# Turning a decoder layer's gated activations with 32x32 block transposes and a way through DRAM instead of TensorE

## The chip, the cores and the metric

The kernel runs on one core of a Trainium2 chip. The metric is the device time of one execution in microseconds; lower is better. The engines are named as in the profile: PE (TensorE, with its weight loads as PEld), DVE (VectorE), ACT (ScalarE), POOL (GpSimd) and SP (SyncE, which here only issues DMAs).

## The reference, cut to what matters

One decoder layer over 256 tokens of width 2048, all in float32. It has two gated feed-forward half-steps, one ahead of and one behind a mixing part (windowed attention and a gated linear recurrence):

```python
def swiglu(h, w_gu, w_down):
    gate, up = jnp.split(h @ w_gu, 2, axis=-1)
    return (jax.nn.silu(gate) * up) @ w_down

x = x + 0.5 * swiglu(rmsnorm(x, ffn1_norm[l]), ffn1_w_gu[l], ffn1_w_down[l])
...                                   # mixing
x = x + 0.5 * swiglu(rmsnorm(x, ffn2_norm[l]), ffn2_w_gu[l], ffn2_w_down[l])
```

The inner width F is 5632. The change touches only what lies between `silu(gate) * up` and the product with `w_down`.

## The kernel before, in words

**Parts.** A float32 matrix product is made of three matmuls in float32r. Each operand is split into a high part (a copy rounded to float32r) and a low part (the rest), and the kernel adds high by high, high by low and low by high. `split_next` (L150, L151) splits the weights: ACT copies `w_raw` to `w_hi`, DVE subtracts to get `w_lo`. The weights come as chunks of 1 MB, 128 x 2048 elements, in a fixed order (`plan`); SP's queue loads them into four `w_raw` buffers, and there are two buffers each of `w_hi` and `w_lo`. `take` hands a chunk to the matmuls and sees to it that the chunk behind it has been split and that four more are on the way. So the split of chunk n+1 can begin when PE has left chunk n-1.

**Projections.** `project` runs over its chunks; for each it goes over the two halves of the tokens (t = 0 and 1, 128 tokens each) and issues 12 matmuls of 512 columns for each half, 24 in a chunk (`mm`, L94). Behind each half it calls `tick()`, so a projection of 8 chunks has 16 ticks. A tick takes one entry of the list `deferred` and runs it; `nothing` is an entry that does nothing. At the end of a projection `flush` runs what is left.

**Feed-forward.** `ffn` has 11 groups of 512 gate and 512 up columns. Each group is one projection `f_gu` of 8 chunks, at the end of which four PSUM banks hold gate and up for the two halves. For each half ACT computes silu of the gate (`sg`, L350) and DVE multiplies with the up part (`act_nat`, L352), tokens on the partitions. The down projection `f_d` needs these activations turned, with the inner width on the partitions, and split into parts (`f_ah`, `f_al`), which stay in SBUF for all 11 groups. `put_later` defers that into the next projection: its first tick does nothing, the second and third each run `put_two`, with four PE transposes of 128x128 into one bank of PSUM (L122), an ACT cast to the high part (L300) and a DVE subtraction to the low part (L301). Behind the last group the next projection is `f_d` itself, whose chunks 20 and 21 of 22 are the first to read that group. There are two feed-forward blocks, `f1` and `f2`, so 22 groups.

**Order.** Instructions are placed on the engines in the order of the program, with a list scheduler that may let one that is ready go ahead of one that waits for data or a buffer; each engine then runs its own in the fixed order that results. `tc.issue_after(ins)` keeps what is issued under it behind `ins` where both are on the same engine; it adds no wait between engines. `last["copy"]` and `last["rest"]` are the latest `w_hi` copy and `w_lo` subtraction that were issued.

**Buffers.** The pool `t2` has six buffers of 128x512 for passing values (`sg`, `act_nat`, the old residual, pieces of the rotary tables and of the mixing part).

Of the kernel before, what the change touches and what calls it, by code (L numbers as in the profile page):

```python
# [8 lines left out]
F32 = mybir.dt.float32  # L9
# [3 lines left out]
ALU = mybir.AluOpType  # L13
AX = mybir.AxisListType

P = 128
D = 2048
S = 256
T = S // P
# [37 lines left out]
def tile_layer(  # L57
# [8 lines left out]
    out = out[0]  # L66
    VE, SC, GP, PE = nc.vector, nc.scalar, nc.gpsimd, nc.tensor
# [10 lines left out]
    def s4(name, dtype=F32, shape=(P, 1024)):  # L78
        return s4p.tile(list(shape), dtype, name=name, tag="s4")

    def t2(name, shape=(P, 512)):
        return t2p.tile(list(shape), F32, name=name, tag="t2")
# [8 lines left out]
    last = {}  # L91
# [76 lines left out]
    deferred, queues = [], []  # L168
# [19 lines left out]
    def plan_project(name, w, c0, ncols, nk):  # L188
        per = 2048 // ncols
        for kc in range(nk // per):  # L190
            src = w[kc * per * P:(kc + 1) * per * P, c0:c0 + ncols].rearrange("(j p) c -> p j c", p=P)
            plan.append((name, [(src, 2048)]))

    def project(name, ncols, nk, xh, xl, near_end=None):

        per = 2048 // ncols
        nb = (ncols + 511) // 512
        wd = min(512, ncols)
        bk = [[bank(f"{name}_{t}_{i}") for i in range(nb)] for t in range(T)]
        chunks = nk // per  # L200
        for kc in range(chunks):
            hi, lo = take(name)
            for t in range(T):
                tok = slice(t * P, (t + 1) * P)

                order = [(range(per), [i]) for i in range(nb)] if kc == chunks - 1 else \
                    [([j], range(nb)) for j in range(per)]
                for js, bs in order:
                    for j in js:
                        k = kc * per + j  # L210
                        ah, al = xh(k)[:, tok], xl(k)[:, tok]
                        cols = {i: slice(j * ncols + i * 512, j * ncols + i * 512 + wd) for i in bs}
                        for i in bs:
                            mm(bk[t][i][:, :wd], ah, hi[:, cols[i]], k == 0, False)
                            mm(bk[t][i][:, :wd], ah, lo[:, cols[i]], False, False)
                        for i in bs:
                            mm(bk[t][i][:, :wd], al, hi[:, cols[i]], False, k == nk - 1)
                tick()
            if kc == chunks - 3 and near_end is not None:
                near_end()  # L220
        flush()
        return bk
# [89 lines left out]
    def put_two(parts, k0, nat, kp, gain=None):  # L312
        ps = trb("put_ps")
        for j in range(2):
            for t in range(T):
                c = (2 * kp + j) * P
                transpose(ps[:, j * S + t * P:j * S + (t + 1) * P], nat[t][:, c:c + P])
        parts.put(k0 + 2 * kp, 2, ps, gain)

    def put_later(parts, k0, nat):  # L320
        deferred.extend([nothing, lambda: put_two(parts, k0, nat, 0), lambda: put_two(parts, k0, nat, 1)])

    def plan_ffn(name, w_gu, w_down):
        guv = w_gu.rearrange("d (h f) -> d h f", h=2)
        for g in range(F // 512):
            for kc in range(KT // 2):
                if not plan:

                    plan.append((f"{name}_gu", [
                        (guv[j * P:(j + 1) * P, h, :512], 512) for j in range(2) for h in range(2)]))  # L330
                    continue
                plan.append((f"{name}_gu", [
                    (guv[(kc * 2 + j) * P:(kc * 2 + j + 1) * P, :, g * 512:(g + 1) * 512], 1024)
                    for j in range(2)]))
        for cg in range(2):
            plan_project(f"{name}_d", w_down, cg * 1024, 1024, F // P)

    def ffn(name, h, old, done):

        act = Parts(f"{name}_act", 0)  # L340
        for g in range(F // 512):
            act.hi.append(s4(f"{name}_ah", F32R, (P, 4, S)))
            act.lo.append(s4(f"{name}_al", F32R, (P, 4, S)))
            bk = project(f"{name}_gu", 1024, KT, h.xh, h.xl)
            nat = []
            for t in range(T):
                gt, ut = bk[t]
                r = h.rstd[:, t:t + 1]
                sg = t2("sg")
                SC.activation(out=sg, in_=gt, func=AF.Silu, scale=r)  # L350
                a = t2("act_nat")
                VE.scalar_tensor_tensor(out=a, in0=ut, scalar=r, in1=sg, op0=ALU.mult, op1=ALU.mult)  # L352
                nat.append(a)
            put_later(act, g * 4, nat)
        for cg in range(2):
            project_residual(f"{name}_d", cg, F // P, act, 0.5, old, done)

    def project_residual(name, cg, nk, parts, scale, old, done):
        res = []

        def fetch():
            for i in range(2):
                q = cg * 2 + i
                res.append([])
                for t in range(T):
                    o = t2("old")
                    nc.sync.dma_start(o, old[t * P:(t + 1) * P, q * 512:(q + 1) * 512])
                    res[i].append(o)

        bk = project(name, 1024, nk, parts.xh, parts.xl, fetch)  # L370
        for t in range(T):
            for i in range(2):
                VE.scalar_tensor_tensor(out=res[i][t], in0=bk[t][i], scalar=scale, in1=res[i][t],
                                        op0=ALU.mult, op1=ALU.add)
        for i in range(2):
            done(cg * 2 + i, res[i])
# [7 lines left out]

    wz = w_in[0]
    plan_ffn("f1", ffn1_w_gu[0], ffn1_w_down[0])
    for name, c, n in (("zf", C_GF, 1024), ("zgq", C_GQ, 1024), ("zgi", C_GI, 1024), ("zkv", C_KV, 256),
                       ("zaq", C_Q, 1024), ("zgo", C_GO, 1024), ("zbA", C_BR, 1024), ("zbA", C_BR + 1024, 1024),
# [5 lines left out]
    for cg in range(2):  # L394
        plan_project("po", w_out[0], cg * 1024, 1024, KT)
    plan_ffn("f2", ffn2_w_gu[0], ffn2_w_down[0])


# [25 lines left out]
    a, v = h1.add(0, xin[0], 0)  # L424
# [123 lines left out]
    def done1(q, pieces):  # L548
        h2.add_later(q, pieces)
        store1(q, pieces)  # L550

    ffn("f1", h1, x, done1)


# [374 lines left out]
    for cg in range(2):  # L929
        bk = project("pa", 1024, 8, ya.xh, ya.xl)  # L930
        for t in range(T):
            for i in range(2):
                c = slice(i * 512, (i + 1) * 512)
                VE.tensor_tensor(out=gA[cg][t][:, c], in0=bk[t][i], in1=gA[cg][t][:, c], op=ALU.mult)
        bk = project("pr", 1024, 8, yh.xh, yh.xl)
        for i in range(2):
            c = slice(i * 512, (i + 1) * 512)
# [14 lines left out]


    ffn("f2", h3, x2, keep(out))


# [47 lines left out]
```

## Time and profile before

| | |
|---|---|
| median of 3 runs | 2131.02 us (2130.55 to 2131.58) |
| the profiled execution's own time | 2130.02 us |
| its span, first to last instruction | 2128.0 us |
| granted TensorE clock | 1.000 of full speed |
| instructions | 23265 |

The profiled execution is 2.0 us longer than its span and 1.0 us shorter than the median. In the trace a matmul's duration covers its way through the array, so matmuls that follow each other overlap, and the distance from start to start tells what one costs.

### The profile page before, as it was taken

The page shows a single profiled execution, that of the slowest core. Times are in us where ns is not written, and L with a number is a line of the kernel's source. Part 1 is how long each engine was busy: PE and PEld are TensorE (multiplying, and loading weights), DVE is VectorE, ACT ScalarE, POOL GpSimd, SP SyncE. Part 2 cuts the span into 40 slices and gives each one's busy share as a digit, 9 for nine tenths or more (in the row PEclk, how much of TensorE's full clock was granted, in tenths as well). Part 3 has the DMA queues.
Part 4 walks back from the last instruction along what each step waited for, and adds up shares of the span by engine and source line. Part 5 has one row for each costly group of instructions (what it writes and reads, how often), then busy time and mean ns, then how long its engine had stood idle before and what let it go on. Part 6 is the DMA issues. An engine that isn't in the chain of part 4 may idle for free.

```text
span 2128.0 us, 23265 instructions
## 1 busy us (share of the span) xinstructions
PE 2121.6 (100%) x9767; PEld 1753.9 (82%) x9767; DVE 1067.4 (50%) x863; ACT 897.2 (42%) x757; POOL 14.4 (1%) x15
## 2 busy tenths in 40 slices
PE   9999999999999999999999999999999999999999
PEld 7888888888888888888788888888888888888887
DVE  5744445444454465446656456554444454444443
ACT  5443333434343355454554433444433434343332
POOL 0000000000000000000100000000000000000000
PEclk9999999999999999999999999999999999999999
DMA  8555555556565565553444555665555555565653
GB/s 289 180 197 179 197 186 190 194 182 225 189 218 196 194 223 178 180 176 139 158 158 158 188 192 183 209 214 182 196 181 195 188 188 197 180 227 190 218 195 119
DMA packets 159711, 405.87 MB, mean 191 GB/s; under 512 B 10276, under 2 KB 13047, under 8 KB 159607
## 3 DMA queue, kind: packets, MB, share of 16 engines
q1 hardware_dynamic: 155830, 397.57, 53.8%
q10 hardware_dynamic: 3776, 6.83, 0.9%
q8 instruction: 76, 1.25, 0.2%
q14 instruction: 29, 0.23, 0.0%
HBM read 398.06 MB, written 6.30 MB: 190 GB/s over the span
## 4 chain that ended last, share of the span: by engine, by line
PE 99%; DMA 0%; ACT 0%; SPq 0%; DVE 0%; issue 0%
PE f_gu L94 45%; PE f_d L94 23%; PE zbR L94 4%; PE zbA L94 4%; PE po L94 4%; PE zgo L94 2%; PE zgq L94 2%; PE zaq L94 2%; PE zgi L94 2%; PE pa L94 2%; PE zf L94 2%; PE pr L94 2%; PE put_ps L122 1%; PE zkv L94 1%; PE h_tp L122 0%; PE pv_ps L94 0%
## 5 line engine op out<-in xcount | busy, mean ns | idle before, releaser
L151 DVE TENSOR_TENSOR w_lo<-w_raw,w_hi 128x2048 fp32r<-128x2048 f32 (+1 forms) x374 | 848.3, 2269 | 953.3 <-ACT w_hi L150 953.1
L150 ACT CAST w_hi<-w_raw 128x2048 fp32r<-128x2048 f32 (+1 forms) x374 | 707.7, 1893 | 1063.0 <-PE f_gu L94 501.7
L94 PE MATMUL f_gu<-w_hi,h_hi 128*128 128x512 f32 x1408 | 552.8, 393 | 0.3 <-ACT w_hi L150 0.3
L94 PE MATMUL f_gu<-w_lo,h_hi 128*128 128x512 f32 x1408 | 548.0, 390 | 0.0
L94 PE MATMUL f_gu<-w_hi,h_lo 128*128 128x512 f32 x1408 | 448.5, 389 | 0.0
L94 PEld LDWEIGHTS f_gu<-w_hi,h_lo 128*128 128x128 f32 x1408 | 264.3, 188 | 55.8
L94 PEld LDWEIGHTS f_gu<-w_hi,h_hi 128*128 128x128 f32 x1408 | 264.3, 188 | 54.2 <-ACT w_hi L150 0.8
L94 PEld LDWEIGHTS f_gu<-w_lo,h_hi 128*128 128x128 f32 x1408 | 264.4, 188 | 53.4
L94 PE MATMUL f_d<-w_hi,f_ah 128*128 128x512 f32 x704 | 274.0, 390 | 0.0
L94 PE MATMUL f_d<-w_lo,f_ah 128*128 128x512 f32 x704 | 273.5, 389 | 0.0
L94 PE MATMUL f_d<-w_hi,f_al 128*128 128x512 f32 x704 | 219.5, 389 | 0.0
L94 PEld LDWEIGHTS f_d<-w_hi,f_al 128*128 128x128 f32 x704 | 132.2, 188 | 27.6
L94 PEld LDWEIGHTS f_d<-w_lo,f_ah 128*128 128x128 f32 x704 | 132.2, 188 | 27.3
L94 PEld LDWEIGHTS f_d<-w_hi,f_ah 128*128 128x128 f32 x704 | 132.1, 188 | 27.0
L94 PE MATMUL zbA<-w_hi,h_hi 128*128 128x512 f32 x128 | 51.8, 406 | 0.0
L94 PE MATMUL zbR<-w_hi,h_hi 128*128 128x512 f32 x128 | 51.7, 407 | 0.0
L94 PE MATMUL po<-w_hi,mT_hi 128*128 128x512 f32 x128 | 50.5, 396 | 0.0
L94 PE MATMUL zbA<-w_lo,h_hi 128*128 128x512 f32 x128 | 49.9, 391 | 0.0
L94 PE MATMUL zbR<-w_lo,h_hi 128*128 128x512 f32 x128 | 49.8, 392 | 0.0
L94 PE MATMUL po<-w_lo,mT_hi 128*128 128x512 f32 x128 | 49.7, 390 | 0.0
L350 ACT ACTIVATE sg<-f_gu,h_rstd 128x512 f32<-128x512 f32 x44 | 30.2, 687 | 30.6 <-PE f_gu L94 30.4
L94 PE MATMUL zbR<-w_hi,h_lo 128*128 128x512 f32 x128 | 41.0, 392 | 0.0
(258 smaller groups left out, 1763.0 us busy)
## 6 DMA issues: line engine op xcount, KB each, us to landing
w_raw<-in_ffn_w_gu SPq DMA_DIRECT2D x350, 512.0 KB, 4.4
w_raw<-in_ffn_w_down SPq DMA_DIRECT2D x88, 1024.0 KB, 4.9
w_raw<-in_w_in SPq DMA_DIRECT2D x74, 1024.0 KB, 4.8
w_raw<-in_w_out SPq DMA_DIRECT2D x16, 1024.0 KB, 5.0
w_raw<-in_w_attn_branch SPq DMA_DIRECT2D x8, 1024.0 KB, 4.8
w_raw<-in_w_hg_branch SPq DMA_DIRECT2D x8, 1024.0 KB, 4.9
x<-old ACTq DMA_DIRECT2D x16, 256.0 KB, 6.5
old<-x SPq DMA_DIRECT2D x16, 256.0 KB, 5.8
```

The costliest lines, as they stand in the source:

```text
L94: last["mm"] = PE.matmul(o, lhsT=lhsT, rhs=rhs, start=start, stop=stop).ins
L122: PE.transpose(out=o, in_=i, identity=ident[:n, :n])
L150: last["copy"] = SC.copy(hi[:, c], raw[:, c]).ins
L151: last["rest"] = VE.tensor_tensor(out=lo[:, c], in0=raw[:, c], in1=hi[:, c].bitcast(F32), op=ALU.subtract).ins
L350: SC.activation(out=sg, in_=gt, func=AF.Silu, scale=r)
```

## The change

The activations of a group are turned without PE. DVE transposes each 32x32 block of `act_nat` in place of the whole 128x128 block, one instruction for each half of the tokens. POOL's queue writes the result to a DRAM tile (256 KB) and reads it back in four transfers of 64 KB, one for each band of 32 partitions, such that the blocks come to lie where a full transpose would have put them; each row of a read is 512 bytes. The parts are then made from the SBUF tile that was read, 128x512 for each half, by an ACT copy and a DVE subtraction. These two are deferred behind nine empty ticks and not one, one half of the tokens in the 10th tick and the other in the 11th, and are kept behind the latest weight split on ACT and on DVE.

```diff
+    def turn(name, nat):
+        blocks = t2(f"{name}_blk", (P, 4, 4, 32))
+        VE.transpose(out=blocks, in_=nat.rearrange("p (q j i) -> p j q i", q=4, j=4))
+        there = tc.dram_tile([P, 512], F32, name=f"{name}_dram")
+        GP.dma_start(there, blocks.rearrange("p j q c -> p (j q c)"))
+        res = t2(f"{name}_T", (P, 4, 4, 32))
+        v = there.rearrange("(g i) (j k) -> j i g k", i=32, j=4)
+        for j in range(4):
+            GP.dma_start(res[j * 32:(j + 1) * 32].rearrange("p g q c -> p g (q c)"), v[j])
+        return res
+
+    def put_turned(parts, k0, t, turned):
+        h, l = parts.hi[k0 // 4], parts.lo[k0 // 4]
+        tok = slice(t * P, (t + 1) * P)
+        h = h[:, :, tok].rearrange("p q (g c) -> p g q c", g=4)
+        l = l[:, :, tok].rearrange("p q (g c) -> p g q c", g=4)
+        with tc.issue_after(last["copy"]), tc.issue_after(last["rest"]):
+            SC.copy(h, turned)
+            VE.tensor_tensor(out=l, in0=turned, in1=h.bitcast(F32), op=ALU.subtract)
...
                 VE.scalar_tensor_tensor(out=a, in0=ut, scalar=r, in1=sg, op0=ALU.mult, op1=ALU.mult)
-                nat.append(a)
-            put_later(act, g * 4, nat)
+                nat.append(turn(f"{name}_a", a))
+            deferred.extend([nothing] * 9 + [lambda t=t, g=g, nat=nat: put_turned(act, g * 4, t, nat[t])
+                                             for t in range(T)])
```

## Rows read from the trace of the kernel before

**Rows 1.** The page's engine table: busy time, share of the span, instructions.
```profile
span 2128.0 us, 23265 instructions
PE 2121.6 (100%) x9767; PEld 1753.9 (82%) x9767; DVE 1067.4 (50%) x863; ACT 897.2 (42%) x757; POOL 14.4 (1%) x15
```

**Rows 2.** The page's chain that ended last, shares by engine.
```profile
PE 99%; DMA 0%; ACT 0%; SPq 0%; DVE 0%; issue 0%
```

**Rows 3.** Waits of PE: waiting line, what it waited for, us, times, longest.
```profile
PE h_tp L122 <- DMA xin<-in_x: 0.6, 1, 0.6
PE f_gu L94 <- ACT w_hi L150: 0.3, 1, 0.3
```

**Rows 4.** Waits of all engines.
```profile
ACT w_hi L150 <- PE f_gu L94: 501.7, 171, 3.9
...
ACT w_hi L150 <- DMA w_raw<-in_ffn_w_gu: 2.7, 2, 2.3
```

**Rows 5.** Waits of SP.
```profile
SPq L137 <- DVE w_lo L151: 1636.0, 345, 9.9
```

**Rows 6.** Timeline of ACT, first block: start, us, instruction, idle before it.
```profile
194.94 1.91 ACT L150 CAST w_hi<-w_raw 128x2048 fp32r<-128x2048 f32 x1 [3.53 <-PE f_gu L94]
...
201.34 1.91 ACT L150 CAST w_hi<-w_raw 128x2048 fp32r<-128x2048 f32 x1 [2.19 <-PE f_gu L94]
206.78 1.91 ACT L150 CAST w_hi<-w_raw 128x2048 fp32r<-128x2048 f32 x1 [3.53 <-PE f_gu L94]
```

**Rows 7.** Instructions on put_ps: duration in ns, min/median/max.
```profile
L122 PE MATMUL put_ps<-ident,act_nat x176: 270/272/273, 61.3 to 1892.5; 128*128 128x128 f32 x176
L300 ACT CAST f_ah<-put_ps x44: 580/584/591, 63.3 to 1892.8; 128x512 fp32r<-128x512 f32 x44
L301 DVE TENSOR_TENSOR f_al<-put_ps,f_ah x44: 680/682/684, 65.6 to 1893.9; 128x512 fp32r<-128x512 f32 x44
```

**Rows 8.** Timeline of PE around one batch of transposes.
```profile
194.28 0.62 PE L94 MATMUL f_gu<-w_hi,h_lo 128*128 128x512 f32 x2
194.74 0.60 PE L122 MATMUL put_ps<-ident,act_nat 128*128 128x128 f32 x4
195.09 0.48 PE L94 MATMUL f_gu<-w_hi,h_hi 128*128 128x512 f32 x1
195.41 0.39 PE L94 MATMUL f_gu<-w_lo,h_hi 128*128 128x512 f32 x1
```

**Rows 9.** Timeline of ACT, second block.
```profile
1533.27 1.91 ACT L150 CAST w_hi<-w_raw 128x2048 fp32r<-128x2048 f32 x1 [3.53 <-PE f_gu L94]
...
1539.68 1.91 ACT L150 CAST w_hi<-w_raw 128x2048 fp32r<-128x2048 f32 x1 [2.18 <-PE f_gu L94]
```

**Rows 10.** Timeline of ACT and DVE where a group ends.
```profile
1837.95 0.74 DVE L352 SCALAR_TENSOR_TENSOR act_nat<-f_gu,h_rstd,sg 128x512 f32<-128x512 f32 x1
...
1839.24 1.91 ACT L150 CAST w_hi<-w_raw 128x2048 fp32r<-128x2048 f32 x1 [0.67 <-PE f_gu L94]
1839.31 0.75 DVE L352 SCALAR_TENSOR_TENSOR act_nat<-f_gu,h_rstd,sg 128x512 f32<-128x512 f32 x1 [0.61 <-PE f_gu L94]
1841.18 2.29 DVE L151 TENSOR_TENSOR w_lo<-w_raw,w_hi 128x2048 fp32r<-128x2048 f32 x1 [1.13 <-ACT w_hi L150]
```

**Rows 11.** Instructions on old: issue in ns min/median/max; last line landing.
```profile
L381 ACTq DMA_DIRECT2D x<-old x16: 326/327/647, 618.2 to 1394.1; - x16
L367 SPq DMA_DIRECT2D old<-x x16: 320/420/648, 1179.6 to 2011.3; - x16
...
DMA to landing us min/median/max: 2.3/6.4/7.4
```

**Rows 12.** Instructions of POOL by line: busy us, mean ns of one, idle before.
```profile
L820 POOL TENSOR_TENSOR a_sc<-a_sc,half_neg 128x16 f32<-128x16 f32 x2 | 6.5, 3230 | 33.7 <-DVE a_sc L819 33.7
...
L272 POOL TENSOR_TENSOR h_rstd<-h_tot,half_neg 128x2 f32<-128x2 f32 x3 | 2.1, 704 | 1080.0 <-DVE h_tot L271 1080.0
```

**Rows 13.** The page's DMA totals.
```profile
DMA packets 159711, 405.87 MB, mean 191 GB/s; under 512 B 10276, under 2 KB 13047, under 8 KB 159607
```

## The prediction

> **What bounds the kernel now.** I read the page's engine table first: of a span of 2128.0 us PE is busy 2121.6, DVE 1067.4 and ACT 897.2 [rows 1]. The chain that ended last is PE for 99% [rows 2]. A busy PE could still be a PE that waits with work queued, so I read its waits next: its only waits for data are 0.6 us for a DMA and 0.3 us for ACT [rows 3]. So PE is never starved: what leaves its stream shortens the span, and anything that starves it lengthens it. Next come the engines that feed it. ACT waited for PE before `w_hi`, 501.7 us in one group alone, but only 2.7 us for weights from DRAM [rows 4]; SP waited 1636 us for DVE to free a `w_raw` buffer [rows 5]. Weights, splits and evictions all run ahead of PE and are paced by it.
>
> The step of that pacing is the chunk: 24 matmuls, then the next `w_hi` copy, which waits for the chunk whose buffer it takes. Without transposes the copies start 206.78 - 201.34 = 5.44 us apart, and across the chunk with the two batches of transposes 201.34 - 194.94 = 6.40 [rows 6].
>
> **What is removed.** `put_two` issues 176 PE transposes for `act_nat` [rows 7]: 22 feed-forward groups (11 in each of two blocks), two batches of four. A transpose shows as 272 ns, but these overlap, so I do not multiply by that. From the first matmul ahead of a batch to the `w_lo` matmul behind it 1.13 us pass [rows 8], where three steps of 5.44/24 = 0.227 us would take 0.68: 0.45 us, or 19.7 us for 44 batches. The copies' spacing also sees the matmuls slowed a little behind a batch: 6.40 - 5.44 = 0.96 us a group, and 1539.68 - 1533.27 = 6.41 shows the same in the second block [rows 9]. I take 0.96: 22 x 0.96 = 21.1 us. The bounds are 19.7 and, for 1.0 us a group, 22.0.
>
> Also gone are 44 `f_ah` casts of 0.58 us and 44 `f_al` subtractions of 0.68 us [rows 7]; their like come back from SBUF. I take the same prices; half or double would not matter, as ACT idles 3.53 us ahead of a split [rows 6] and DVE works 2.29 us of each 5.44 [rows 10]. That idle time is the cover.
>
> **What is added at the group's end: 44 DVE transposes.** Call the start of a new group's first chunk 0; in [rows 10] that is 1839.2. DVE ends the two `act_nat` at -0.5 and 0.9 and begins `w_lo` of chunk 1 at 2.0. No row shows a 32x32-block transpose. Lower bound: 0.57 us, the rate of `w_lo` (2.29 us for 2048 elements) times 512. Upper bound: 1.5 us, twice the slower 512-element instruction (0.75). I take 0.75, as it is one pass over the same 512. Then the first runs from -0.5 to 0.24, the second `act_nat` ends at 1.0 and the second transpose at 1.74: `w_lo` is not delayed. If they take T, the second ends at 2T + 0.24. The chain from `w_hi` to the end of `w_lo` is 1841.18 + 2.29 - 1839.24 = 4.23 us; PE wants `w_lo` 0.23 us into chunk 1, at 5.67, so 1.44 us are spare and PE stalls only for T over 1.6 us. Both bounds cost nothing.
>
> **The way through DRAM: 44 writes and 176 reads, issued by POOL.** For each half of the tokens 256 KB go out, and four 64 KB reads that wait for the landing come back. POOL's queue is otherwise empty here, SP's and ACT's get nothing new, so behind a waiting POOL instruction stand only this group's other transfers. Landing: 6.4 us, the median of 256 KB tiles, with bounds 2.3 and 7.4 [rows 11]. The price of a POOL issue, c, is not in the trace. Bounds: 0.32 us, SP's fastest issue [rows 11], and 3.27, POOL's longest instruction [rows 12]. I take 1.1, POOL's shortest tensor instruction (0.70) plus an SP issue (0.42) [rows 11, 12]. The first half: ready 0.24, written by 0.24 + 1.1 + 6.4 = 7.7, reads issued by 12.1, landed 18.5. The second: its write is issued at 1.74 to 2.84, its reads behind the first half's from 12.1 to 16.5, landed 22.9. The Trainium skill (DMA: Bandwidth & Descriptors, section Latency and other measured facts) puts the first byte of a GpSimd-issued DMA at about 1 us; no row here shows one, and by 1.0 us an issue the second half would land at 22.0 and the total would be the same.
>
> **When they are needed.** The pair that `put_turned` issues sits at the 10th and 11th tick, the end of chunk 4 and the middle of chunk 5. On ACT the first copy is behind the split of chunk 5 (21.8 to 23.7), the second behind that of chunk 6 (27.2 to 29.1). Behind each on ACT is the next split, at 27.2 and 32.6, and behind that PE; on DVE the subtraction stands ahead of the next `w_lo`, which waits for the same split. With a copy of 0.6 us and the 1.44 us to spare PE is starved only if a half lands after 28.0 or 33.4. The estimates are 9.5 and 10.5 us earlier, so nothing stalls: cost 0. Without that cover each microsecond of lateness costs 22 us. Chunk 20 of the down projection, which reads the last group, is far later.
>
> **Traffic.** 44 x 0.524 = 23 MB on 405.9 [rows 13], 6%. Weights have slack: SP waits for buffers, not ACT for weights [rows 4, 5]. Cost 0. The `t2` buffers now stay taken until chunk 5, which can hold up the rotary tables once in the first block: 0 to 2 us, I take 0.
>
> **Sum.** The profiled execution took 2130.0 us, 2.0 more than its span and 1.0 less than the median of 2131.0. 2130.0 - 21.1 = 2108.9, and from the median 2109.9. I predict 2110 us, 2107 to 2113 in this case. A change under 0.2% (4.3 us) could not be told from none.
>
> **Rivals.**
>
> 1. Slower: the second half lands late. Place: ACT's second `put_turned` copy, with the split of chunk 7 and then PE behind it. Landing is at 0.24 + c + 6.4 + 8c + 6.4 = 13.0 + 9c, so it decides from c = 2.26 us. At 2.5 it is 2.1 us late: 22 x 2.1 = 47, giving 2157; at 3.27 it is 9.1 us late, giving 2310. If the second write were queued behind the first half's reads, 19.4 + 10c would decide from 1.4 us. For it: ten issues that no row prices, two landings in series. Against: the slowest issues in [rows 11] take 0.65 us, so c would have to be over three times that. Chance 0.12.
>
> 2. Slower: DVE shuts POOL out while `w_lo` runs. `w_lo` occupies 2.29 of each 5.44 us, from 2.0, 7.4, 12.9, 18.3 and 23.7. Issues fitted into the gaps at 1.1 us bring the second half at 29.2, still in time; at 2.0 us they bring it at 36.4, 3.0 us late: 66 us, giving 2176. The trace has no POOL work beside `w_lo` that could show it. The Trainium skill (SBUF — State Buffer, section SBUF: two separate sides) says that a DMA issued by GpSimd starves for descriptors while DVE runs in a two-port mode, and that fp32 copies between SBUF tiles trigger it. The trace speaks against such a mode for `w_lo`: from `f_al`'s 0.68 us for 512 elements, read from PSUM, to 2.29 us for 2048 an element costs 1.05 ns, no less than in `f_al` itself to within its fixed part [rows 7, 10]. Chance 0.05.
>
> 3. Partly eaten: a half is late by up to 0.7 us a group, or the block transpose takes up to 2.0 us (0.8 us a group, 18 us): 2113 to 2127. Chance 0.12.
>
> 4. No change: the time is not given back, since the PE stream then runs into the splits. Against: the chain takes 4.23 of 5.44 us. 2127 to 2135. Chance 0.05.
>
> **Chances and range.** My forecast has 0.66. Faster is 0.66 + 0.12 = 0.78, same 0.05, slower 0.12 + 0.05 = 0.17. The range runs from 2107 to 2128: forecast, third rival and the edge of the fourth, some 0.8; the bounds 19.7 and 22.0 lie inside.
>
> **What would show it.** Right: no `put_ps` from `act_nat`, PE instructions down from 9767 to 9591, `w_hi` starts 5.44 us apart through each group's first chunks, PE's waits still near 2 us, `put_turned` copies that start as soon as their split ends, DVE transposes that end ahead of `w_lo`. Wrong: ACT waiting for DMA ahead of `f_ah`, POOL issues over 2.2 us, or `w_hi` and `w_lo` as releasers of PE. Then the loss per group times 22 is the miss.

## The result, and the profile after

The changed kernel takes 2109.52 us (median of four runs, 2109.14 to 2110.16), the kernel before 2130.78 us (four runs, 2130.30 to 2131.58). The ratio is 0.990, with a 95% interval from 0.9887 to 0.9912: 21.3 us, or 1.0%, faster. The forecast was 2110 us.

The profiled execution after, first the page's engine table, chain and DMA lines:

```profile
span 2107.4 us, 23475 instructions
...
PE 2100.6 (100%) x9591; PEld 1736.6 (82%) x9591; DVE 1097.3 (52%) x907; ACT 892.4 (42%) x756; POOL 135.2 (6%) x235
...
DMA packets 168866, 428.98 MB, mean 204 GB/s; under 512 B 13795, under 2 KB 16566, under 8 KB 168758
...
PE 100%; ACT 0%; DVE 0%; POOL 0%; issue 0%; POOLq 0%; ACTq 0%
```

Against [rows 1], PE has 176 instructions fewer and is busy 21.0 us less (2121.6 to 2100.6); the span is 20.6 us shorter. DVE has 44 instructions more and 29.9 us more work, POOL 220 more and 120.8 us more. Neither is seen in the end: the chain is PE still, as in [rows 2]. Against [rows 13] the traffic has grown by 23.1 MB (428.98 from 405.87).

The view of waits, for PE (waiting line, what it waited for, us, times, longest), answers [rows 3]:

```profile
PE warm L435 <- POOL ident masks.py:199: 1.4, 1, 1.4
PE f_gu L94 <- ACT w_hi L150: 0.5, 1, 0.5
```

Beside these there is one wait of 0.4 us for the first input: in 2107 us PE waits 0.5 us for a split. The timeline of ACT through a group's first chunks answers [rows 6]; each line is start, duration, instruction, and the idle time before it with its releaser:

```profile
186.90 1.91 ACT L150 CAST w_hi<-w_raw 128x2048 fp32r<-128x2048 f32 x1 [2.94 <-PE f_gu L94]
188.72 0.68 ACT L374 ACTIVATE sg<-f_gu,h_rstd 128x512 f32<-128x512 f32 x1
...
208.66 1.91 ACT L150 CAST w_hi<-w_raw 128x2048 fp32r<-128x2048 f32 x1 [3.53 <-PE f_gu L94]
210.47 0.61 ACT L344 CAST f_ah<-f_a_T 128x512 fp32r<-128x512 f32 x1
214.10 1.91 ACT L150 CAST w_hi<-w_raw 128x2048 fp32r<-128x2048 f32 x1 [3.01 <-PE f_gu L94]
215.91 0.61 ACT L344 CAST f_ah<-f_a_T 128x512 fp32r<-128x512 f32 x1
219.54 1.91 ACT L150 CAST w_hi<-w_raw 128x2048 fp32r<-128x2048 f32 x1 [3.01 <-PE f_gu L94]
```

The four chunks from 186.90 to 208.66 take 21.76 us, 5.44 each; the one step of 6.40 is gone. The two `f_ah` copies start as soon as their splits end, with no idle time ahead of them, and the next splits still idle 3.01 us for PE: the data had been there.

DVE and POOL in the same group (for POOL, the issuing instructions; "x4" are four reads in a row):

```profile
186.40 0.71 DVE L328 STREAM_TRANSPOSE f_a_blk<-act_nat 128x512 f32<-128x512 f32 x1
188.85 2.29 DVE L151 TENSOR_TENSOR w_lo<-w_raw,w_hi 128x2048 fp32r<-128x2048 f32 x1 [1.74 <-ACT w_hi L150]
191.06 0.75 DVE L376 SCALAR_TENSOR_TENSOR act_nat<-f_gu,h_rstd,sg 128x512 f32<-128x512 f32 x1
191.84 0.71 DVE L328 STREAM_TRANSPOSE f_a_blk<-act_nat 128x512 f32<-128x512 f32 x1
```

```profile
187.40 0.56 POOL L330 DMA_DIRECT2D f_a_dram<-f_a_blk  x1 [29.27 <-DVE f_a_blk L328]
192.37 2.18 POOL L334 DMA_DIRECT2D f_a_T<-f_a_dram  x4 [4.41 <-issue]
194.54 0.56 POOL L330 DMA_DIRECT2D f_a_dram<-f_a_blk  x1
198.98 2.18 POOL L334 DMA_DIRECT2D f_a_T<-f_a_dram  x4 [3.87 <-issue]
```

The second half's `act_nat` and transpose do not stand ahead of `w_lo`, as I had them, but behind it, and the second write stands behind the first half's reads. The silu it waits for has moved too: ACT runs the second half's `sg` at 188.72, behind the split, where in the group of [rows 10] it ran at 1837.88, ahead of the split at 1839.24. It is so in every group; why the scheduler places it there was not followed up. The view of the tile that was read back gives all 176 reads: their issue in ns (min/median/max) and the time to landing. The `f_al` subtraction from it takes 686 ns in the median.

```profile
L334 POOL DMA_DIRECT2D f_a_T<-f_a_dram x176: 548/551/572, 61.7 to 1881.9; - x176
...
DMA to landing us min/median/max: 2.1/4.0/7.5
```

### The profile page after: what moved, and what is told of

The parts are those of the page before. It is cut to its first block, busy times and chain, and to the rows that moved or that the text cites. A ratio compares the mean times of both kernels' runs of the same rounds, so it can differ in the third digit from the quotient of the medians.

```text
span 2107.4 us, 23475 instructions
## 1 busy us (share of the span) xinstructions
PE 2100.6 (100%) x9591; PEld 1736.6 (82%) x9591; DVE 1097.3 (52%) x907; ACT 892.4 (42%) x756; POOL 135.2 (6%) x235
## 2 busy tenths in 40 slices
DMA packets 168866, 428.98 MB, mean 204 GB/s; under 512 B 13795, under 2 KB 16566, under 8 KB 168758
## 4 chain that ended last, share of the span: by engine, by line
PE 100%; ACT 0%; DVE 0%; POOL 0%; issue 0%; POOLq 0%; ACTq 0%
PE f_gu L94 46%; PE f_d L94 23%; PE zbR L94 4%; PE zbA L94 4%; PE po L94 4%; PE zgo L94 2%; PE zgq L94 2%; PE zaq L94 2%; PE zgi L94 2%; PE pa L94 2%; PE zf L94 2%; PE pr L94 2%; PE zkv L94 1%; PE pv_ps L94 0%; PE h_tp L122 0%; PE o_ps L94 0%
## 5 line engine op out<-in xcount | busy, mean ns | idle before, releaser
L334 POOL DMA_DIRECT2D f_a_T<-f_a_dram x176 | 96.0, 552 | 193.8 <-issue 127.0
L330 POOL DMA_DIRECT2D f_a_dram<-f_a_blk x44 | 25.0, 568 | 641.4 <-DVE f_a_blk L328 641.4
```

The lines of the kernel that those rows point to most:

```text
L330: GP.dma_start(there, blocks.rearrange("p j q c -> p (j q c)"))
L334: GP.dma_start(res[j * 32:(j + 1) * 32].rearrange("p g q c -> p g (q c)"), v[j])
```

## Experiments

The theory: the whole gain is PE time that left the stream, and everything added is hidden, with some 10 us to spare in a group. The rivals: the way through DRAM costs something that another gain hides; the spare time or the order is not needed, so that the long deferral and the tie do nothing; POOL's queue or DVE's load sets the landing. "Before" and "after" below are the two kernels' medians, 2130.8 and 2109.5 us; the ratios are to runs of the kernel before beside each experiment, whose medians were 2130.5 to 2130.8 us.

**The PE work back, the rest kept.** The 176 PE transposes are issued again at the ticks where they used to be, into PSUM that nobody reads; the parts still come by way of DRAM.

```diff
...
-            deferred.extend([nothing] * 9 + [...])
+            deferred.extend([nothing, lambda raw=raw: idle_two(raw, 0), lambda raw=raw: idle_two(raw, 1)]
+                            + [nothing] * 6 + [...])
```

> The changed kernel with PE's 176 transposes put back as well, into a PSUM bank that nobody reads; DVE's block transposes, the way through DRAM and the parts stay. The transposes of a group now stand eight in a row. Theory (the whole gain is PE time): four in a row take 0.35 us and slow the matmul behind them by about 0.1, so eight cost 0.8 to 0.96 us a group, 22 groups 17.6 to 21.1: 2127 to 2131 us. Rival (the gain came from the casts and subtractions that no longer read PSUM, or from freed PSUM banks): the time stays near 2109.5, at most 2115.

Measured: 2131.77 us (2131.31 to 2132.89), ratio to before 1.0006 [0.9996, 1.0015]. The engine table:

```profile
PE 2122.1 (100%) x9767; PEld 1753.6 (82%) x9767; DVE 1097.4 (52%) x907; ACT 892.5 (42%) x756; POOL 135.2 (6%) x235
```

The time is that of before again, with DVE's and POOL's new work still there. 22.3 us over after is 1.01 us a group, and PE's busy time grows by 21.5. So all of the gain is these transposes, at under half of what 4 x 2 x 272 ns = 2.18 us a group would say.

**The way left out, the rest kept.** No block transpose, no write, no reads: the parts are made of `act_nat` as it is. This leaves out the turning of the activations, so the down projection multiplies other numbers of the same shape.

```diff
-                nat.append(turn(f"{name}_a", a))
+                nat.append(a.rearrange("p (g q c) -> p g q c", g=4, q=4))
```

> The changed kernel without block transposes and without the way through DRAM: the parts are made straight from the activations that were not turned (so the product that follows is of other numbers), still in the 10th and 11th tick. Theory (the way is hidden whole): 2109.5 us, within 2 us. Rival (the way costs something and the gain would have been larger): below 2105 us, by 0.2 us a group or more.

Measured: 2109.79 us (2109.19 to 2110.20), 0.9902 [0.9887, 0.9917]. The engine table:

```profile
PE 2102.3 (100%) x9591; PEld 1738.4 (82%) x9591; DVE 1067.9 (51%) x863; ACT 894.9 (42%) x756; POOL 14.4 (1%) x15
```

Taking away 29.4 us of DVE work, 120.8 us of POOL's and 23 MB gives back nothing: the median is 0.3 us higher, inside the runs' spread. The cost of 0 for the way stands.

**Fewer empty ticks.** The same kernel with 6 and with 4 empty ticks ahead of the pair, in place of 9.

```diff
-            deferred.extend([nothing] * 9 + [...])
+            deferred.extend([nothing] * 6 + [...])     # the other run: * 4
```

> The parts after 6 empty ticks in place of 9. ACT has both copies between the splits of chunks 4 and 5, from 18.2 us after the group's start; the second half lands at 18.3, the next split is due at 21.8. Theory: nothing is late, 2109.5 us within 2 us. Rival (the 9 steps are needed, as a landing is often far later than the median): 2115 us or more.

> The parts after 4 empty ticks in place of 9; nothing else is changed. ACT then has both copies between the splits of chunks 3 and 4. By the profile of the changed kernel the second half lands some 18.3 us after the group's start, so its copy ends at 18.9, the split of chunk 4, due at 16.3, is 2.6 us late, 1.44 of that is spare, and 1.2 us a group are lost: theory of a cover that is used up: 2109.5 + 22 x 1.2 = 2136 us, 2125 to 2150 as the landing varies by half a microsecond and more. Rival (the steps do not matter, the way lands at once or the wait is hidden anyway): 2109.5 us.

With 6: 2111.64 us (2111.35 to 2112.41), 0.9912 [0.9897, 0.9926], 2.1 us over after and so a little past the 2 us I had allowed; PE's one wait for a split at a block's end makes 0.4 us of that, and the rest was not located. With 4: 2139.07 us (2137.37 to 2141.24), 1.004 [1.0025, 1.0055], slower than before. With 6, ACT waits for the reads three times: at the end of each block and behind the second block's first group. Its timeline at the first block's end (the group starts at 492.54):

```profile
515.54 0.62 ACT L344 CAST f_ah<-f_a_T 128x512 fp32r<-128x512 f32 x1 [4.24 <-DMA f_a_T<-f_a_dram]
```

The second half lands there at 515.54 - 492.54 = 23.0 us, and not at about 18; at the other two places it lands 22.3 and 22.7 us after the start. With 4, ACT waits for the reads 25 times, and PE waits too (the views of waits of both engines):

```profile
ACT f_ah L344 <- DMA f_a_T<-f_a_dram: 96.2, 25, 10.0
...
PE f_d L94 <- ACT w_hi L150: 8.7, 2, 4.7
PE f_gu L94 <- DVE w_lo L151: 4.2, 6, 1.8
PE f_gu L94 <- ACT w_hi L150: 3.2, 2, 2.6
```

The total came out about as I expected (29.6 us over after, where I had 26), but it is made up otherwise. I had 1.2 us in each of 22 groups. The waits say 7.4 us in eight waits within the blocks (`f_gu`), 4.4 of them in two (2.6 and 1.8) behind the first group of the second block; and 11.8 us at the two blocks' ends (`f_d`: 8.7, and 3.1 more for `w_lo`). An ordinary group, from the timeline of ACT (start 1489.08):

```profile
1501.78 0.61 ACT L344 CAST f_ah<-f_a_T 128x512 fp32r<-128x512 f32 x1
1506.70 0.62 ACT L344 CAST f_ah<-f_a_T 128x512 fp32r<-128x512 f32 x1 [4.31 <-DMA f_a_T<-f_a_dram]
1507.23 1.91 ACT L150 CAST w_hi<-w_raw 128x2048 fp32r<-128x2048 f32 x1
```

The second copy waits until 1506.70, 17.6 us after the start, and the split behind it, due at 1499.96 + 5.44 = 1505.40, starts 1.83 us late; with 1.44 us to spare that is some 0.4 us for PE, which waits 0.5 us there. Only five ordinary groups show such a wait, of 0.4 to 0.6 us. This is the queueing behind a waiting instruction that the prediction told of, with its price. The other 10.5 us are in PE's busy time (2111.1 against 2100.6). Stretches of PE around the first block's end (busy us, instructions, granted clock, DMA share, GB/s) show where a part of it lies:

```profile
510.00:515.00 5.00, 4.43 (x20) 1.00 0.90 282
515.00:520.00 5.00, 0.80 (x1) 0.67 0.23 74
520.00:525.00 5.00, 4.25 (x10) 0.50 0.60 203
525.00:530.00 5.00, 5.00 (x19) 0.81 0.54 216
```

PE waits 4.0 us there for `w_hi` and, one matmul later, 1.5 us for `w_lo`; in these stretches the granted clock is 0.67, 0.50 and 0.81, on its way back to 1.00. At 0.50 (1.2 of 2.4 GHz) PE was busy for 4.25 us with 10 instructions, 0.43 us each; at 1.00 they follow each other every 0.227 us. From 515 to 530 there are 29 instructions in 10.04 busy us, 3.5 more than 29 x 0.227; the same count gives 1.6 us behind the second block's first group (1465 to 1470) and 2.0 at the second block's end (1905 to 1920). So by this estimate some 7 of the 10.5 us lie where the clock is low. The rest was not located; PE's busy time differs by 1.7 us even between after and the run without the way (2102.3), which take the same time.

**No tie.** The copies may go ahead of the splits on ACT and DVE; the nine empty ticks stay.

```diff
-        with tc.issue_after(last["copy"]), tc.issue_after(last["rest"]):
-            SC.copy(h, turned)
-            VE.tensor_tensor(out=l, in0=turned, in1=h.bitcast(F32), op=ALU.subtract)
+        SC.copy(h, turned)
+        VE.tensor_tensor(out=l, in0=turned, in1=h.bitcast(F32), op=ALU.subtract)
```

> The changed kernel without keeping the parts behind the latest split. ACT's order is then: split of chunk 2, first half's copy, split of chunk 3, second half's copy, split of chunk 4. Theory (what matters is where the copies stand among ACT's splits, and the tie puts them two chunks later): as with 4 empty ticks, the second half lands at 18.3 and the split of chunk 4 is 1.8 to 2.6 us late: 2125 to 2150 us. Rival (the 9 empty ticks alone put them late enough): 2109.5 us.

Measured: 2130.07 us (2128.74 to 2134.31), 1.0000 [0.9991, 1.0009]: the whole gain is gone. The timeline of ACT in the group that was shown above, here with its start at 189.82:

```profile
200.91 0.62 ACT L343 CAST f_ah<-f_a_T 128x512 fp32r<-128x512 f32 x1 [3.75 <-DMA f_a_T<-f_a_dram]
201.44 1.91 ACT L150 CAST w_hi<-w_raw 128x2048 fp32r<-128x2048 f32 x1
```

The list scheduler has put the copies into the queue more than two chunks earlier than with the tie: they start 11.1 and 16.6 us after the group (23.6 and 29.0 with it), and only then because they wait for the reads. All 44 copies of the run wait so, and splits stand behind them. The two longest lines of PE's waits behind that of ACT, and one stretch of PE (columns as above):

```profile
ACT f_ah L343 <- DMA f_a_T<-f_a_dram: 166.2, 44, 7.7
...
PE f_d L94 <- DVE w_lo L151: 5.1, 4, 1.8
PE f_gu L94 <- DVE w_lo L151: 3.5, 5, 1.8
```

```profile
1450.00:1460.00 10.00, 7.06 (x23) 0.83 0.43 131
```

All of PE's waits for splits make 11.7 us, and PE's busy time is 9.7 us over that of after (2110.3). In the stretch shown, at the first group of the second block, and in one at that block's end the granted clock is 0.83 in the mean. By 0.227 us an instruction these two are 3.4 us too long; the other 6.3 us were not located. Most groups get by on the spare 1.44 us, a few do not. So the nine empty ticks alone do not keep the gain. The deferral counts only as far as the instructions also stand late in their engine's queue.

**Sixteen reads for four.** Each read is cut into four of 16 KB, 704 reads.

```diff
-            GP.dma_start(res[j * 32:(j + 1) * 32].rearrange("p g q c -> p g (q c)"), v[j])
+            for g in range(4):
+                GP.dma_start(res[j * 32:(j + 1) * 32, g].rearrange("p q c -> p (q c)"), v[j][:, g])
```

> Each of the four reads of a half cut into four, so 16 reads of 16 KB in place of 4 of 64 KB: POOL issues 748 transfers and not 220. With the 0.55 us that an issue takes in the changed kernel the second half's reads are issued until about 28 us after the group's start and land at about 32, where PE is starved only for a landing after 33.4. Theory (POOL's issues in a row set the landing): both copies on ACT now wait for their reads, but in an ordinary group PE does not; at the two ends of a block, where the weights of the down projection load the DMA engines and a landing is some 5 us later, it does by 3 to 4 us: 2110 to 2122 us. Rival (the transfers themselves are the cost, the issue is not): the landing and the time stay as they are, 2109.5 us.

Measured: 2129.28 us (2112.31 to 2135.09 in ten runs, an unusually wide spread), 0.9992 [0.9973, 1.0011]. I had expected at most 2122. In the profiled execution the tile's reads are issued in 0.50 us each (median 496 ns), and the waits of PE are these:

```profile
PE f_d L94 <- ACT w_hi L150: 8.2, 2, 4.6
PE f_d L94 <- DVE w_lo L151: 3.4, 2, 1.8
...
PE f_gu L94 <- ACT w_hi L150: 0.4, 1, 0.4
```

All of these waits but 0.4 us are at the two blocks' ends (`f_d`); the ordinary groups stood the 12 further issues a half, as the theory had it. What I had not counted shows in POOL's timeline at the first block's end (the group starts at 492.66):

```profile
498.02 3.92 POOL L335 DMA_DIRECT2D f_a_T<-f_a_dram  x8 [4.29 <-issue]
502.58 3.91 POOL L335 DMA_DIRECT2D f_a_T<-f_a_dram  x8 [0.64 <-DMA f_a_T<-f_a_dram]
508.59 0.58 POOL L330 DMA_DIRECT2D f_a_dram<-f_a_blk  x1 [2.10 <-DMA f_a_T<-f_a_dram]
516.83 3.92 POOL L335 DMA_DIRECT2D f_a_T<-f_a_dram  x8 [7.67 <-ACT w_hi L150]
...
528.38 1.96 POOL L335 DMA_DIRECT2D f_a_T<-f_a_dram  x4 [2.70 <-issue]
```

POOL stopped between runs of its own reads until earlier ones had landed (42 such waits, 40.7 us in all), and the DMA engines were nearly full in places (a share of 0.94 from 505 to 510 and of 1.03, by the view, from 520 to 525). The second half landed at 531.89 - 492.66 = 39.2 us, 5.8 us past the 33.4 that the prediction gave as the limit; the `f_d` waits of PE come to 8.2 + 3.4 = 11.6 us, 5.5 of them at this end. Behind them the granted clock is 0.53 (535 to 540), and PE's busy time in the whole run is 8.5 us over that of after. So the limit is real; that it was crossed only at the blocks' ends is what the runs show, but how the pauses and the fuller DMA engines share in it was not separated.

**SP's queue for POOL's.** All writes and reads are issued by SP, between the loads of the weights.

```diff
-        GP.dma_start(there, ...)
+        nc.sync.dma_start(there, ...)
...
-            GP.dma_start(res[...], v[j])
+            nc.sync.dma_start(res[...], v[j])
```

> The writes and reads issued by SP in place of POOL; weight loads then stand behind SP's waits for a landing. A wait is some 4.5 us for each half, a weight chunk is asked for some 16 us ahead of its split and lands in 4 to 5. Theory (weights have that slack): 2109.5 us, 2108 to 2113. Rival (POOL's empty queue is what hides the way; behind SP the weights come late): 2120 us or more, with ACT waiting for w_raw.

Measured: 2109.65 us (2109.18 to 2110.03), 0.9901 [0.9884, 0.9917], no different from after. The tile's view:

```profile
L334 SPq DMA_DIRECT2D f_a_T<-f_a_dram x176: 307/426/1877, 60.8 to 1881.5; - x176
```

ACT's waits for weights from DRAM come to 9.4 us in five (5.5 us after, 2.7 in [rows 4]), and PE has none but at the start: the weights run far enough ahead that transfers waiting in their queue are not felt. A queue of their own is not what makes the change work.

**More work on DVE.** 16 further copies of 128x512 on DVE for each group, to see whether a busy DVE holds POOL's issues up (the second rival).

```diff
+    def spare_copies():
+        for i in range(2):
+            VE.tensor_copy(out=spare, in_=csb[:, :512])
...
-            deferred.extend([nothing] * 9 + [...])
+            deferred.extend([spare_copies] * 8 + [nothing] + [...])
```

> 16 spare DVE copies of 128x512 float32 from SBUF to SBUF are added to each group, spread over its first chunks, the time in which POOL issues its transfers. Theory (DVE's work does not hold up POOL's issues enough to matter): POOL's issues stay near 0.55 us, the time within 3 us of 2109.5. Rival (a DVE copy in a two-port mode shuts POOL out, as the Trainium skill's page SBUF — State Buffer says in its section SBUF: two separate sides): issues grow by the length of a copy, some 0.3 to 0.6 us each, the landing moves by up to 6 us, and copies wait on DVE for POOL; even so PE is not starved in an ordinary group.

Measured: 2118.95 us (2118.39 to 2119.59), 0.9945 [0.993, 0.996]; I had expected it within 3 us of after, and it is 9.4 over. The copies and POOL's issues, from the views of their tiles:

```profile
L340 DVE COPY spare<-csb x352: 381/427/514, 31.6 to 339.5; 128x512 f32<-128x512 f32 x176
```

```profile
L335 POOL DMA_DIRECT2D f_a_T<-f_a_dram x176: 548/551/773, 66.1 to 1892.5; - x176
```

The copies depend on nothing, so the list scheduler ran all 352 in the first 340 us and packed DVE with them. A stretch of this kernel (busy us and instructions of PE, PEld, DVE, ACT, POOL; granted clock, DMA share, GB/s), and then the same stretch of the changed kernel:

```profile
150.00:200.00 50.00, 49.84 (x217) 39.88 (x216) 48.42 (x76) 19.77 (x15) 6.29 (x11) 1.00 0.66 216
```

```profile
150.00:200.00 50.00, 50.00 (x222) 41.43 (x221) 24.86 (x16) 20.15 (x14) 8.07 (x15) 1.00 0.70 229
```

DVE is busy 48.4 of 50 us and PE does 217 instructions where it did 222. The view of waits of PE's weight loads names the wait, which the changed kernel does not have:

```profile
PEld f_gu L94 <- DVE w_lo L152: 11.5, 27, 1.4
```

So the loss is DVE that has no room left for `w_lo`. POOL's issues are not to blame: of the 176 reads 48 are issued between 60 and 330 us, where DVE is 97% busy, with a median of 550 ns, the longest 0.2 us longer than any in the changed kernel, and they land in 3.7 us in the median, as in the same stretch of the changed kernel. The run answers its question; its own time I had misjudged, since I took it that the copies would stay in their ticks.

**More of the same change.** The first 1024 channels of the second and third normed input (`h2`, `h3`) and the first 1024 columns of the mixing part's `mT` are turned by way of DVE and DRAM as well; 48 PE transposes more, in 12 batches, are gone. It ran beside the changed kernel.

```diff
+            def second(q, t):
+                g = self.g[:, 4 * q:4 * q + 4].unsqueeze(1).unsqueeze(3).broadcast_to([P, 4, 4, 32])
+                r = self.early[q][t]
+                with tc.issue_after(last["rest"]):
+                    VE.tensor_tensor(out=r, in0=r, in1=g, op=ALU.mult)
+                put_split(self.hi[:, 4 * q:4 * q + 4, :], self.lo[:, 4 * q:4 * q + 4, :], t, r)
...
+                early = [turn("m_a", gA[cg][t][:, c]) for t in range(T)]
+                queues.append([later_parts(i * 4, early, 11 + 2 * i)])
```

> The changed kernel with three more places turned by DVE and DRAM: the first 1024 channels of the normed input of the mixing part and of the second feed-forward block (they are finished one projection before they are read), and the first 1024 columns of the merged branches. 48 PE transposes go, 12 batches of four; DVE gets 12 block transposes and 8 multiplications by the gains, POOL 60 transfers. Theory (each batch is worth 0.48 us of PE time as long as its parts are ready): 12 x 0.48 = 5.8 us, 2103.7 us, 2102 to 2106. Rival (in these places the landing or the extra work of ACT and DVE stands in front of a split, as in the experiment with 4 empty ticks): 2109 us or more.

> The changed kernel itself, beside the version with more places turned, on the same chip: 2109.5 us, within 1 us.

Measured: 2105.59 us (2105.12 to 2106.22), 0.9883 [0.9868, 0.9898]; the changed kernel beside it 2109.88 (2109.09 to 2110.53), 0.9903 [0.9886, 0.9919]. The gain is 4.3 us of the 5.8 expected. The engine table, and PE's longest wait behind the start:

```profile
PE 2096.1 (100%) x9543; PEld 1731.5 (82%) x9543; DVE 1108.1 (53%) x919; ACT 890.7 (42%) x748; POOL 167.5 (8%) x295
```

```profile
PE f_gu L94 <- DVE w_lo L151: 1.3, 1, 1.3
```

PE's busy time falls by a further 4.5 us, and against that stand 1.5 us in two waits for `w_lo` (1.3 and 0.2 us) that the changed kernel does not have. It is the fastest version of the study, though the intervals of the two ratios overlap; the runs themselves, 2105.12 to 2106.22 against 2109.09 to 2110.53, do not.

## Why the prediction was right

**PE's term.** 21.1 us were forecast; PE's busy time fell by 21.0, the median by 21.3, and putting the transposes back cost 22.3. The choice that mattered was to read the price from the spacing of `w_hi` [rows 6] and not from the transposes' own duration: 176 x 272 ns would have said 47.9 us, and the gap around a batch in [rows 8] 19.7 (0.45 x 44 is 19.8).

**PE takes the gain at once.** The fourth rival (no change) is out: no new releaser of PE, spacing 5.44 us.

**The block transpose.** 0.71 us, where 0.75 was taken.

**The order at the group's end.** This step was wrong, and harmless; it was one of the prediction's own signs of being right, and that sign failed. I had both transposes ahead of `w_lo` of chunk 1. In the trace the second half comes behind it, and its transpose ends 191.84 + 0.71 - 186.90 = 5.65 us after the start, not 1.74. `w_lo` was not delayed by it, as the forecast said, but because it went first. POOL's queue had the order write, reads, write, reads, the one that the first rival priced as its worse case.

**The way's length.** POOL's issue was over-sized, 0.55 us for 1.1, and so was the landing, 4.4 and 3.9 us for the writes and 4.0 for the reads, for 6.4. In the worse order that gives 1.06 + 4.4 + 2.18 + 0.56 + 3.9 + 2.18 + 4.0 = 18.3 us for the second half, where 22.9 was forecast, and the first half's reads are issued by 7.6 and have landed by 11.6, for 18.5. In the run with four empty ticks an ordinary group's second half was there at 17.6 us.

With the landings it assumed, the first rival needed 1.4 us an issue in this order, and the issue took 0.55. The Trainium skill (DMA: Bandwidth & Descriptors, Latency and other measured facts) puts the first byte of a GpSimd-issued DMA at about 1 us; the issue here takes 0.55 us and the landing 4 us, so the trace neither needs nor excludes that figure.

**When they are needed.** The copies stand at 23.6 and 29.0 us after the start, forecast 23.7 and 29.1, and have no idle time ahead of them. The limit and the spare 1.44 us are borne out by the run with four empty ticks (1.8 us late, about 0.4 lost) and by the sixteen reads (past the limit, PE waits). What the forecast lacked is that three of the 22 groups, the last of each block and the first of the second, are slower by 4 to 5 us: at the first block's end the second half lands 23.0 us after the start (run with six empty ticks), and the DMA engines' share there is 1.00 and 0.96 in the changed kernel's stretches 500 to 505 and 505 to 510. That this is so near the forecast 22.9 is chance, since neither the issues, the landings nor the order were those of the forecast. Even so 10 us were left.

**The second rival,** DVE shutting POOL out, is answered by the run with the spare copies: 0.2 us at most. The Trainium skill (SBUF — State Buffer, SBUF: two separate sides) says that DVE's two-port copies between SBUF tiles in fp32 starve a GpSimd-issued DMA of descriptors. These were such copies, 0.43 us for the 512 elements for which the block transpose takes 0.71. Neither the issues nor the landing of 3.7 us beside them show the starving, so by that measurement the rule does not hold for this pair of operations, at copies of this length.

**Traffic, the two copies, `t2`.** 23.1 MB, 0.61 and 0.69 us for 0.58 and 0.68, no wait of PE; DVE waits 0.7 us once, at the first of the rotary tables' work (`turns`), for a write of the way. All is as costed. The run without the way, which keeps the two copies, shows that the block transposes and the traffic cost nothing that can be told from the runs' spread.

**Misses among the experiments.** The transposes put back cost 22.3 us where I had at most 21.1, and six ticks 2.1 us where I had at most 2. The larger ones are the time of the spare copies, the time of the sixteen reads, and the make-up of the four-tick run and of the one without the tie. With the sixteen reads I had the place right, but took 3 to 4 us at a block's end where it was 5.5 and 6.1, and left out the lower clock behind it. The last two have one cause: I priced lateness as microseconds a group, where the spare 1.44 us swallow most of it in ordinary groups and the waits at the blocks' ends and in the second block's first group cost their length and the lower clock behind them.

## What to carry to other kernels

Where PE is busy all through and its feeders run ahead, price work that leaves it by the spacing of a periodic instruction with and without that work, not by its own duration, and ask of what replaces it only whether it is there in time. Work moved to another engine and back by DRAM was free here because its readers stood late enough in their queues; deferring them in the program was not enough under the list scheduler, they had to be tied behind the urgent work. Check the margin at the slowest place (here a block's end, 5 us later than the others), since a long starving there cost its length and clock behind it, while the spare time of an ordinary group swallowed most of its lateness.

## What the runs showed of the hardware

- Two waits of PE of 4.0 and 1.5 us, one matmul apart, came with a granted clock of 0.50 (1.2 of 2.4 GHz) in the stretch 520 to 525, and 0.81 in the next, in the run with four empty ticks. By the estimate above that and two like places added some 7 us of busy time to 19.2 us of waits. In the run without the tie two waits of 1.3 and 1.8 us, one soon behind the other, were followed by 0.76 in the stretch 1455 to 1460.
- POOL issues a 64 KB transfer in 0.55 us and a 16 KB one in 0.50, so the issue's cost hardly depended on the bytes; SP took a median of 0.43 for the same 64 KB.
- With sixteen reads a half POOL paused for the landing of its own earlier reads, 42 times.
